# Five of eight loads moved from Sync's DMA queue to GpSimd's software queue in a 3-D average pooling kernel

## Chip, cores and metric

One NeuronCore of a Trainium2 chip. The metric is the device time of one execution in microseconds (us). Times are medians of several runs in the fast state, with a granted clock of 1.0, apart from x8_late_store, a single run whose state is unknown.

## The reference

```python
def setup_inputs():
    batch, channels, d, h, w = (8, 32, 32, 32, 32)
    kernel_size = 2
    return {'x': np.random.randn(batch, channels, d, h, w).astype(np.float32), 'kernel_size': kernel_size}

# cut here: reference() loops over i, j, k; in short:
# result[:, :, i, j, k] = mean of the 2 x 2 x 2 window of x at (2i, 2j, 2k)
```

The input is 256 rows (batch x channels) of 128 KiB, 33.55 MB; the output is an eighth of that, 4.19 MB.

## The kernel before

Each group of 128 rows fills the 128 partitions. A load brings 16, 32 or 48 KiB of every row into a slot of one ring buffer; the vector engine (DVE) then adds along d, along w and along h. Slots are reused, so some loads must wait until DVE has finished with the slot. DVE reports its progress by a count: one for each tile's first addition, one for its second and one for the read at its end, so three a tile.

```python
    plan = [                 # (row group, first KiB, KiB, slot in the ring)
        (0, 0, 32, 0),
        (0, 32, 48, 32),
        (0, 80, 48, 80),
        (1, 0, 32, 128),
        (1, 32, 32, 0),
        (1, 64, 32, 32),
        (1, 96, 16, 64),
        (1, 112, 16, 80),
    ]
    # ... pool_unit: three DVE operations and one read of an accumulator
    for t, k0, kb, r0 in plan:
        unit = ring[:, r0 * KF:(r0 + kb) * KF]
        nc.sync.dma_start(out=unit, in_=xv[t * P:(t + 1) * P, k0 * KF:(k0 + kb) * KF])
        pool_unit(unit, t, k0, kb)

    for t, k0, kb in [(0, 0, 16), (1, 0, 12), (1, 12, 4)]:
        nc.sync.dma_start(out=ov[...], in_=obuf[t][...])
```

After the program is built, it is edited: the first store is held back until one DVE count before the second store's (17 instead of what its data needs), and the first load is moved ahead of the opening barrier.

```python
    need, = [w for w in second.sync_info.on_wait if w.ant_name.startswith("DVE")]
    # ... in the first store's waits:
            w = copy.replace(w, wait_value=need.wait_value - 1)
```

## Time and profile before

| | before |
|---|---|
| time, median | 91.19 us (91.16 to 91.21, 3 runs) |
| span of the profile | 88.0 us |
| DVE busy | 63.2 us |
| DMA queue, share of 16 engines | 99.1% |
| last load landed / last store landed | 80.1 / 89.9 us |

"Landed" is the last of the 16 semaphore counts that the DMA engines post for a transfer. The span ends with the last instruction, before the last store has landed. In the windows view used below, a row gives a stretch of time and its length, DVE's busy time and instructions, GpSimd's (POOL), the granted clock, the mean busy share of the 16 DMA engines, and GB/s. (A packet is counted in the stretch where it starts, so a share can pass 1.) Here is its tail before:

```profile
69.60:73.40 3.80, 3.03 (x1) 0.00 (x0) 1.00 1.03 440
73.40:78.00 4.60, 4.53 (x3) 0.00 (x0) 1.00 1.00 427
78.00:80.00 2.00, 2.00 (x3) 0.00 (x0) 1.00 0.98 418
80.00:85.00 5.00, 4.90 (x6) 0.00 (x0) 1.00 1.01 431
```

The reader should see the second-last column: the engines never rest, through the last loads and over the change to stores near 80.

### The profile page before, as it was taken

To read this page: it belongs to the slowest core of one execution; us is meant where nothing else is said; L and a number is where in the kernel's file an instruction comes from. 1 tells how busy PE (TensorE), PEld (TensorE's weight loads), DVE (VectorE), ACT (ScalarE), POOL (GpSimd) and SP (SyncE) were. 2 spreads that over 40 slices of the span, in tenths; PEclk is the share of its full clock that TensorE was granted. 3 is DMA by queue.
4 is the path that set the end of the run, shared out by engine and by line. 5 is a ranking of instruction groups with operands and counts; after the bars stand their busy time and mean duration, and the time that the engine had idled before them with its cause. 6 is when DMAs were issued, how large, how long until landed. Compare 5 with 4: busy or idle time off the path is not lost.

```text
span 88.0 us, 78 instructions
## 1 busy us (share of the span) xinstructions
DVE 63.2 (72%) x32; POOL 0.2 (0%) x4
## 2 busy tenths in 40 slices
DVE  0000049991008999942999999999999299999994
POOL 0000000000000000000000000000000000000000
DMA  8979999888998889986999988999989999999999
GB/s 238 462 328 402 477 402 670 358 358 358 536 536 358 358 358 603 469 358 298 417 477 477 477 358 358 477 477 477 402 358 432 417 417 462 402 447 440 410 434 400
DMA packets 1440, 37.26 MB, mean 424 GB/s; under 512 B 152, under 2 KB 152, under 8 KB 160
## 3 DMA queue, kind: packets, MB, share of 16 engines
q1 hardware_dynamic: 1440, 37.26, 99.1%
HBM read 33.55 MB, written 4.19 MB: 429 GB/s over the span
## 4 chain that ended last, share of the span: by engine, by line
DMA 66%; DVE 32%; issue 0%; DVEq 0%
DMA ring<-in_x_dram 66%; DVE ring L60 18%; DVE ring L65 9%; DVE obuf L68 5%; DVE dummy L68 0%; DVEq L91 0%
## 5 line engine op out<-in xcount | busy, mean ns | idle before, releaser
L60 DVE TENSOR_TENSOR ring<-ring 128x4096 f32<-128x4096 f32 (+2 forms) x8 | 35.4, 4422 | 23.0 <-DMA ring<-in_x_dram 23.0
L65 DVE TENSOR_TENSOR ring<-ring 128x2048 f32<-128x2048 f32 (+2 forms) x8 | 18.3, 2292 | 0.3
L68 DVE CUSTOM_DVE_ANT_1 obuf<-ring 128x1024 f32<-128x1024 f32 (+2 forms) x8 | 9.8, 1225 | 0.3
L68 DVE DVE_READ_ACCUMULATOR2_ANT dummy<- 128x1 f32 x8 | 0.7, 82 | 0.0
L183 POOL MEMSET const-bfloat16-1.0<- 128x1 bf16 x1 | 0.1, 103 | 0.0
L183 POOL MEMSET const-uint8-127<- 128x1 uint8 x1 | 0.1, 102 | 0.0
L183 POOL MEMSET const-float32-0.0<- 128x1 f32 x1 | 0.1, 100 | 0.2 <-issue 0.2
L183 POOL MEMSET const-float32-1.0<- 128x1 f32 x1 | 0.1, 99 | 0.0
## 6 DMA issues: line engine op xcount, KB each, us to landing
ring<-in_x_dram SPq DMA_DIRECT2D x4, 4096.0 KB, 36.2
ring<-in_x_dram SPq DMA_DIRECT2D x2, 6144.0 KB, 32.9
ring<-in_x_dram SPq DMA_DIRECT2D x2, 2048.0 KB, 32.7
out_dram<-obuf SPq DMA_DIRECT2D x1, 2048.0 KB, 7.9
out_dram<-obuf SPq DMA_DIRECT2D x1, 1536.0 KB, 10.2
out_dram<-obuf SPq DMA_DIRECT2D x1, 512.0 KB, 3.1
```

What stands on the lines that cost most here:

```text
L60: first = nc.vector.tensor_add(out=b.rearrange("p (o e) -> p o e", o=od), in0=a[:, :, 0], in1=a[:, :, 1])
L65: nc.vector.tensor_add(out=c, in0=bv[:, :, 0], in1=bv[:, :, 1])
L68: nc.vector.tensor_tensor_reduce(out=obuf[t][:, o0:o0 + od * 256].rearrange("p (j k) -> p j k", k=16), in0=cv[:, :, 0], in1=cv[:, :, 1], s ...
L183: nc = _bacc.Bacc("TRN2", target_bir_lowering=False, num_devices=1)
```

## The change

Its intent, as I read it, is to give each of the five middle loads one large packet per DMA engine instead of eight. I call the first load of SP (the Sync engine) H0 (32 KiB a row), GpSimd's five S0 to S4 (48, 48, 32, 32, 32 KiB), and SP's last two H1 and H2 (16 KiB each).

```diff
     plan = [
-        (0, 0, 32, 0),
-        (0, 32, 48, 32),
-        (0, 80, 48, 80),
-        ...
+        (0, 32, 48, 32, False),      # S0, now first on DVE
+        (0, 0, 32, 0, True),         # H0, still issued first
+        (0, 80, 48, 80, False),      # S1
+        (1, 0, 32, 128, False),      # S2
+        (1, 32, 32, 0, False),       # S3, in H0's slot
+        (1, 64, 32, 32, False),      # S4, in S0's slot
+        (1, 96, 16, 64, True),       # H1
+        (1, 112, 16, 80, True),      # H2
     ]
...
+        if hw:
+            nc.sync.dma_start(out=unit, in_=src)
+        else:
+            nc.gpsimd.dma_start(out=unit, in_=src, single_packet=True)
...
+    n, load = loads[1]               # H1
+            w = copy.replace(w, wait_value=14)   # its wait for DVE, raised to count 14
```

So three things change at once: the queue, DVE's order of the first two tiles, and a raised wait of H1.

More of the change, by code (lines that the diff above doesn't have):

```diff
@@ L44, in pool_rows @@
     plan = [
-        (0, 0, 32, 0),
-        (0, 32, 48, 32),
-        (0, 80, 48, 80),
-        (1, 0, 32, 128),
-        (1, 32, 32, 0),
-        (1, 64, 32, 32),
-        (1, 96, 16, 64),
-        (1, 112, 16, 80),
+        (0, 32, 48, 32, False),
[6 more added lines that the diff above has]
+        (1, 112, 16, 80, True),
     ]
@@ L72, in pool_unit @@
         )
-    for t, k0, kb, r0 in plan:
+    for t, k0, kb, r0, hw in plan:
         unit = ring[:, r0 * KF:(r0 + kb) * KF]
-        nc.sync.dma_start(out=unit, in_=xv[t * P:(t + 1) * P, k0 * KF:(k0 + kb) * KF])
+        src = xv[t * P:(t + 1) * P, k0 * KF:(k0 + kb) * KF]
+        if hw:
+            nc.sync.dma_start(out=unit, in_=src)
+        else:
+            nc.gpsimd.dma_start(out=unit, in_=src, single_packet=True)
         pool_unit(unit, t, k0, kb)
@@ L93 @@
     program = blocks[tc.starting_block_idx].instructions
+    loads = [
+        (n, i) for n, i in enumerate(program)
+        if isinstance(i, mybir.InstDMACopy) and "in_" in i.ins[0].memref
+        and i.engine == nc.sync.engine]
+    assert len(loads) == 3
+    n, load = loads[1]
+    waits = []
+    for w in load.sync_info.on_wait:
+        if w.ant_name.startswith("DVE"):
+            assert w.wait_value < 14
+            w = copy.replace(w, wait_value=14)
+        waits.append(w)
+    program[n] = copy.replace(load, sync_info=mybir.SyncInfo(
+        on_wait=waits, on_update=load.sync_info.on_update))
     stores = [
@@ L113 @@
     opening = blocks[0].instructions
-    load = next(i for i in program if isinstance(i, mybir.InstDMACopy))
+    load = next(
+        i for i in program if isinstance(i, mybir.InstDMACopy) and i.engine == nc.sync.engine)
     assert load.engine == nc.sync.engine
```

## The prediction

> **What bounds the kernel now.** I read the page first (busy share of the vector engine DVE, and the share of the 16 DMA engines), then the timeline (when each tile's first addition could start, which is when its load had landed), then the chain that ended last. The page:
>
> ```profile
> DVE 63.2 (72%) x32; POOL 0.2 (0%) x4
> ...
> q1 hardware_dynamic: 1440, 37.26, 99.1%
> HBM read 33.55 MB, written 4.19 MB: 429 GB/s over the span
> ```
>
> One queue keeps all 16 DMA engines busy for 99.1% of the 88.0 us span; DVE needs 63.2 us. So DMA is the bound. The reader should see in the third column of the queue line that no idle is left to remove: only bytes, packet overhead or the ends of the run can give time back.
>
> The timeline shows the landings, as the ends of DVE's idle times:
>
> ```profile
> 12.14 4.42 DVE L60 TENSOR_TENSOR ring<-ring 128x4096 f32<-128x4096 f32 x1 [12.14 <-DMA ring<-in_x_dram]
> ...
> 26.65 6.56 DVE L60 TENSOR_TENSOR ring<-ring 128x6144 f32<-128x6144 f32 x1 [6.49 <-DMA ring<-in_x_dram]
> ...
> 41.21 6.56 DVE L60 TENSOR_TENSOR ring<-ring 128x6144 f32<-128x6144 f32 x1 [2.81 <-DMA ring<-in_x_dram]
> ...
> 70.37 4.42 DVE L60 TENSOR_TENSOR ring<-ring 128x4096 f32<-128x4096 f32 x1 [1.54 <-DMA ring<-in_x_dram]
> ```
>
> From 12.14 to 26.65 one load of 128 x 48 KiB (6.29 MB) lands: 434 GB/s. From 41.21 to 70.37 three loads of 128 x 32 KiB (12.58 MB) land in 29.16 us: 432 GB/s. The stream has no holes. The chain that ended last has this tail:
>
> ```profile
> 38.43 31.91 DMA ring<-in_x_dram
> 70.35 0.02 issue
> 70.37 4.43 DVE ring L60
> ...
> 82.58 2.22 DVE ring L60
> 84.80 0.02 issue
> 84.83 1.24 DVE ring L65
> 86.06 0.02 issue
> 86.08 0.69 DVE obuf L68
> ```
>
> After the sixth load lands at 70.35, DVE works without a break to 86.78 on three tiles. The last store (0.5 MB, issued at 86.8, 3.1 us to landing) ends at 89.9; the median time, 91.19, is 1.3 later. Meanwhile DMA is full too (the trace's semaphore landings: last load 80.1, stores 85.0, 88.7, 89.9), so the DVE tail and the byte stream end nearly together.
>
> **What the Trainium skill says.** (1) "DMA: Bandwidth & Descriptors", section "Issuing engines are not separate DMA queues": DMAs from Sync and GpSimd run on the same 16 engines and interleave, so a second queue adds no bandwidth. The trace agrees in so far as one queue already fills 99.1%. (2) Same page, "Queues, rings and completion order": each engine round-robins between the rows with work, a whole packet at a time. The trace before has one queue, so nothing shows it; this decides the rivals below. (3) Same page, "Why small descriptors are slow (HBM only)": a fixed overhead of some 3 cycles per packet. The trace agrees in kind: its packets of 16,384, 32,768 and 49,152 bytes take 611, 1213 and 1815 ns (medians). The slope, (1815-611)/32768, is 27.2 GB/s; what is left over is about 9 ns a packet. (4) "SBUF — State Buffer", "Who interferes with whom": GpSimd's descriptor writing is locked out by DVE's two-port modes, and the page infers that a tensor_tensor doesn't lock it out, because that takes only the shared read side. No GpSimd DMA has run yet, so no run shows it.
>
> **The change part by part.** Bytes, tiles and DVE instructions are the same: the instruction order shows 33 working DVE rows in another order (the 48-KiB tile first, the 32-KiB tile second), five loads moved from SP to GpSimd.
>
> Removed: packet boundaries. A load has 128 rows, 8 per engine, so 8 packets an engine become 1. Five loads x 7 packets x 9 ns = 0.3 us per engine. That is all that the byte stream can gain.
>
> Removed and added issue time: five issues of 0.33 to 0.52 us on SP become GpSimd's. Each lies under a 10 to 14 us transfer, so 0.
>
> Moved: SP's first load (call it H0) still starts before the barrier at 0.00, first packet at 1.02. GpSimd's first load (S0, 48 KiB rows) can be issued after the barrier, about 0.8 (SP's second load was at 0.80 before). I allow 2 to 3 us for software descriptors, my estimate. By 4.0 H0 has done about two of its eight rows (the first took 1.7 to 2.2 us in the trace, later ones 1.22). Then S0's single packet holds each engine for 8 x 1.806 = 14.45 us.
>
> My main line supposes that H0 then gets its six rows before S1, as the changed DVE order implies. Landing is 0.4 us after the last byte, as before. Tile times from the timeline: 48 KiB 11.7 us (26.65 to 38.40), 32 KiB 7.9 (52.88 to 60.81), 16 KiB 4.2 (78.30 to 82.50).
>
> - S0 lands 18.9, H0 26.2, S1 40.6, S2 50.3.
> - DVE: S0 18.9 to 30.6, H0 30.6 to 38.5, S1 40.6 to 52.3, S2 52.3 to 60.2.
> - S3 reuses H0's slot: issued at 38.5, well before S2 has left the engines (49.9), lands 60.0. S4 reuses S0's slot and lands 69.6.
> - DVE: S3 60.2 to 68.1, S4 69.6 to 77.5.
> - The penultimate SP load now waits for the 14th DVE count. Three counts per tile (the first store before waited for count 17 and started at 77.15, as the sixth tile's second addition ended), so 14 is S3's second addition, about 66.9. That is 2.4 us before S4 leaves the engines at 69.3: just in time. The last two loads land about 74.6 and 79.5, DVE ends 85.9.
> - Stores: 2, 1.5 and 0.5 MB behind the loads, last landing about 89.5, against 89.9.
>
> Sum: 91.19 minus 0.3 for packets, perhaps 0.1 more or less at the start: 90.8. The DVE tail gets about 0.9 us of air (85.9 against 86.8), but the byte stream then sets the end, so that air isn't gained.
>
> **The rivals.**
>
> A. Strict alternation of one packet per queue. H0's rows are packets of 32 KiB, S0 to S2 packets of 384, 384 and 256 KiB an engine. H0 then gets one row after S0, one after S1, and the rest after S2: it lands near 50. DVE, in program order, idles from 30.6 to 50; S3 is issued only at 58. DVE from 50 on has 7.9 + 11.7 + 7.9 x 3 + 4.2 x 2 = 51.7 us: ends near 102, last store 3.1 later, plus 1.3: about 106. For it: the skill's words on round robin. Against it: the changed wait at count 14 would then fall near 84, with DMA idle since about 70; nobody who saw that trace would set it there, while in my main line it fits to 2 us. That is an argument from the design, not a measurement.
>
> B. The queues share by bytes, or H0 goes first entirely. S0 lands at 25 (equal shares: 604 KiB left of both at 27.2 GB/s from 3 us) or 26.6 (H0 first). DVE starts there and has 63.4 us: ends 88.5 to 90.0, plus 3.1 plus 1.3: 93 to 94.4, slower by 2 to 3.5%. DVE becomes the bound. For it: DVE's start moves from 12.1 to 18.9 at best, so only about 4 us of DVE slack is left (23.0 us of idle before, of which 18.9 is now spent before the first addition). Against it: the reordering would make no sense.
>
> C. Software descriptors are slower: a gap of a microsecond between two GpSimd packets, or a descriptor write held up by DVE. Five gaps of 1 us add up to 5 us at most; but other queued work can fill part. I think 0 to 2 us.
>
> D. Faster by more than 2%: needs under 89.4. At the pure slope of 27.2 GB/s an engine (435 GB/s) 37.75 MB take 86.8 us; with 1.0 to the first packet, 0.4 to land and 1.3 after, that is 89.5 with every packet overhead gone. So practically excluded.
>
> **Range and chances.** Main line 90.8 (about 70%, with C's small gaps up to 92), B about 10%, A about 12%, C large about 8%. I put the prediction at 91.0 and the range at 90.4 to 93.5; A lies outside. Faster by over 2%: 0.02; within 2% (89.4 to 93.0): 0.74; slower: 0.24.
>
> **What would show it.** Right: two DMA queues with about 25 MB on the software one and a joint share near 99%; DVE's first addition near 19, second tile without a long wait (landing by 27 to 31); single software packets of about 14.4 us; the last two loads issued near 67; DVE ending near 86. Wrong by A: DVE idle some 20 us before the second tile, DMA share falling between 50 and 60. Wrong by B: first addition at 25 or later and an unbroken DVE after it. Wrong by C: the DMA share a few per cent lower in the middle slices, with idle DVE before the third and later tiles. The prediction is wrong altogether if engines deliver more than 27.2 GB/s in single packets, for which the trace shows no sign.

## The result

| | before | after |
|---|---|---|
| time, median | 91.20 us (91.16 to 91.26, 4 runs) | 97.06 us (96.94 to 97.09, 4 runs) |
| DVE busy | 63.2 us | 63.1 us |
| DVE starts its first addition | 12.14 us | 26.44 us |
| S4 landed (sixth load before) | 70.35 us | 70.07 us |
| last load landed | 80.1 us | 85.9 us |
| last store landed | 89.9 us | 95.7 us |

The ratio is 1.064, 95% interval 1.0621 to 1.0658. Ratios here are the mean time of one kernel's fast runs over that of the other's of the same rounds, so not quite the ratio of the medians quoted. Executions over 1.5% slower than the fastest of the same kernel are left out of the means.

The page after:

```profile
DVE 63.1 (69%) x32; POOL 3.0 (3%) x9
...
q0 software_dynamic: 720, 25.17, 63.8%
q1 hardware_dynamic: 635, 11.21, 31.1%
HBM read 33.55 MB, written 4.19 MB: 413 GB/s over the span
```

The two queues together keep the engines busy for 94.9% of the span instead of 99.1%. The software queue carried exactly its 25.17 MB, in 720 packets: 5 loads x 128 rows is 640 data packets, plus 80 semaphore writes. In spite of the one-packet flag, the records show every row by itself. (A row is one partition's piece of a load, 8 of them per engine; it is not the queue row of the skill's page.)

Where does DVE start? The timeline after:

```profile
26.44 6.56 DVE L60 TENSOR_TENSOR ring<-ring 128x6144 f32<-128x6144 f32 x1 [26.44 <-DMA ring<-in_x_dram]
...
38.11 4.42 DVE L60 TENSOR_TENSOR ring<-ring 128x4096 f32<-128x4096 f32 x1
```

Only the first addition has a bracket: DVE waits for 26.44 us, and from then on data are there, apart from 0.14 us before H2's tile near 85.9. In the trace's landings H0 was complete at 22.8, before S0 at 26.4, but DVE takes S0 first. How the queues shared is in the DMA view after, for the stretch from 7 to 20 us (packets, MB, share):

```profile
q0 software_dynamic: 64, 3.15, 55.9%
q1 hardware_dynamic: 66, 2.16, 38.5%
```

In that stretch 64 rows of S0 and 66 of H0 began: one row for one row. The bytes differ only because S0's rows are 48 KiB and H0's 32.

And the end of the chain that ended last, after (start, us, what):

```profile
70.10 2.30 DVE ring L65
72.40 0.02 issue
72.42 0.33 SPq L78
...
72.87 13.04 DMA ring<-in_x_dram
85.90 0.02 issue
85.93 2.30 DVE ring L60
```

Count 14 comes at 72.4 with the end of the fifth tile's second addition (L65). Only then SP issues H1 and H2, and H2 takes 13.0 us to land. The windows after show what that does to DMA:

```profile
69.60:73.40 3.80, 3.73 (x3) 0.00 (x0) 1.00 0.07 17
73.40:81.00 7.60, 7.53 (x5) 0.00 (x0) 1.00 1.00 405
81.00:85.00 4.00, 3.97 (x4) 0.00 (x0) 1.00 0.97 287
```

Two losses stand here, to be held against the same stretch of the kernel before. From 69.6 to 73.4 DMA runs dry (17 GB/s): S4's last row ends at 69.63 and H1's first begins at 73.38. And from 81 to 85 the engines are "busy" but move only 287 GB/s: rows of 16 KiB, every one of which took 0.611 us in the kernel before, take up to 1.32. A busy share near 1 is thus not a full rate. DVE is hardly held up by this: it ends at 90.2, and the last store is issued at 90.24. But the stores stand behind the late loads, so this store takes 5.4 us to land instead of 3.1.

### The profile page after: what moved, and what is told of

Its sections match the earlier page's. It is cut to its first block, busy times and chain, and to the rows that moved or that the text cites. A ratio compares the mean times of both kernels' runs of the same rounds, so it can differ in the third digit from the quotient of the medians.

```text
span 91.3 us, 78 instructions
## 1 busy us (share of the span) xinstructions
DVE 63.1 (69%) x32; POOL 3.0 (3%) x9
## 3 DMA queue, kind: packets, MB, share of 16 engines
q0 software_dynamic: 720, 25.17, 63.8%
## 4 chain that ended last, share of the span: by engine, by line
DVE 55%; DMA 42%; issue 1%; SPq 0%; PEldq 0%; DVEq 0%
DMA ring<-in_x_dram 42%; DVE ring L60 31%; DVE ring L65 16%; DVE obuf L68 7%; SPq L78 0%; DVE dummy L68 0%; PEldq L95 0%; DVEq L95 0%
## 5 line engine op out<-in xcount | busy, mean ns | idle before, releaser
L60 DVE TENSOR_TENSOR ring<-ring 128x4096 f32<-128x4096 f32 (+2 forms) x8 | 35.4, 4423 | 26.6 <-DMA ring<-in_x_dram 26.4
L65 DVE TENSOR_TENSOR ring<-ring 128x2048 f32<-128x2048 f32 (+2 forms) x8 | 18.3, 2293 | 0.3
L80 POOL DMA_DIRECT2D ring<-in_x_dram x5 | 2.7, 554 | 44.3 <-DVE dummy L68 43.4
## 6 DMA issues: line engine op xcount, KB each, us to landing
ring<-in_x_dram SPq DMA_DIRECT2D x1, 4096.0 KB, 22.8
```

Of the source, the lines that this page charges most:

```text
L60: first = nc.vector.tensor_add(out=b.rearrange("p (o e) -> p o e", o=od), in0=a[:, :, 0], in1=a[:, :, 1])
L65: nc.vector.tensor_add(out=c, in0=bv[:, :, 0], in1=bv[:, :, 1])
L80: nc.gpsimd.dma_start(out=unit, in_=src, single_packet=True)
```

## The experiments

My theory after the result (Theory 1): rows of the two queues alternate, so S0 lands at 26.4; DVE starts there because its order puts S0 first; the late DVE makes the count-14 wait late, and DMA runs dry. Rivals: the software queue is slow by itself (Theory 2), or the one-packet flag sets how the queues share (Theory 3). The first eight runs below were made on one chip and the last two on another, each beside runs of the kernel before on the same chip.

### x1_tile_order: DVE takes H0 first

```diff
     plan = [
-        (0, 32, 48, 32, False),
         (0, 0, 32, 0, True),
+        (0, 32, 48, 32, False),
```

> The changed kernel with one thing undone: DVE takes the 32-KiB tile (SP's first load) first and the 48-KiB tile (GpSimd's first load) second; all loads, queues and the count-14 wait stay. Theory 1 (the loss is the DVE order: GpSimd's rows alternate with SP's, so the tile that DVE waits for lands at 26.4 instead of 18.9): DVE starts near 22.8, fourteenth count near 68.7, so no hole before the last two loads, end near 91.0. Theory 2 (the software queue itself is slow): little gained, 95 or more.

Measured: 93.74 us (93.4 to 93.85, 5 fast runs; a sixth, 95.04, counts as slow), ratio to before 1.0271 (1.0254 to 1.0289). DVE starts at 22.88 and count 14 comes at 68.86, both as expected. So the hole all but closes, and 3.3 us come back. But the expected 91.0 was missed by 2.7. The windows of this run say where:

```profile
69.60:73.40 3.80, 3.66 (x3) 0.00 (x0) 1.00 0.97 349
73.40:78.00 4.60, 4.53 (x3) 0.00 (x0) 1.00 0.99 424
78.00:82.00 4.00, 3.93 (x5) 0.00 (x0) 1.00 1.02 328
```

DMA restarts at 69.84 after a pause of 0.1 us or more on each engine, and its first rows cost 0.56 us more than usual per engine (349 GB/s). Then from 78 to 82 there are slow rows again (1.0 us per engine in the packet records). H2 lands at 82.7 instead of 80.1.

### x2_gate12: H1 waits for count 12 instead of 14

```diff
-            w = copy.replace(w, wait_value=14)
+            w = copy.replace(w, wait_value=12)
```

> The changed kernel with the wait of SP's second load lowered from DVE count 14 to 12. Theory 1: DVE still starts at 26.4 and works without a break, the two loads are issued at 65.7 instead of 72.4, the hole of 3.8 us in the DMA stream goes, DVE ends near 89.8 and the last store ends the run 3.1 later: 94.2. That splits the loss of 5.9 into some 3 for the start and some 3 for the wait. Theory 2 (software queue): about 97 still.

Measured: 94.14 us (94.1 to 94.34, 4 runs), ratio 1.0326 (1.0307 to 1.0345). It came out as Theory 1 said, to 0.1 us. H1 is issued at 65.9, the loads end by 80.0 without slow rows, and DVE, which started at 26.57, sets the end. The stretch that ran dry in the changed kernel (0.07, 17 GB/s) is full here:

```profile
69.60:73.40 3.80, 3.73 (x3) 0.00 (x0) 1.00 1.06 453
```

The last store is issued at 90.14, only 0.1 us earlier than in the changed kernel, but lands 2.7 us later and not 5.4: what the late wait costs is paid in the queue of stores, not in DVE's time. Theory 2 in its simple form (about 97 still) falls.

### x4_many_packets: without the one-packet flag

```diff
-            nc.gpsimd.dma_start(out=unit, in_=src, single_packet=True)
+            nc.gpsimd.dma_start(out=unit, in_=src)
```

> The changed kernel without the one-packet flag on the five GpSimd loads. Theory 1 (the flag doesn't make a packet hold an engine; rows of the two queues alternate either way): first tile lands at 26 again, time 97.1 plus at most 0.3, rows of 49,152 bytes at 1.815 us again. Theory 3 (the flag sets how the queues share): another landing order or time, by 1 us or more.

Measured: 96.90 us (96.82 to 97.01, 4 runs), ratio 1.0625 (1.0609 to 1.0641). Its DMA view from 7 to 20 us:

```profile
q0 software_dynamic: 64, 3.15, 55.8%
q1 hardware_dynamic: 65, 2.13, 37.9%
```

Row for row again, 64 to 65. Median rows took 1.815 us (48 KiB) and 1.213 us (32 KiB) with the flag and without it. So the flag neither holds an engine nor saves the time between rows here, and Theory 3 falls. Whether the flag took effect in the descriptors at all, the records do not show: they have 720 packets on this queue either way. S2 to S4 landed 9.71 us apart with the flag and 9.73 without.

### x5_before_48_first: the tile order alone, on SP's queue

```diff
-    for t, k0, kb, r0 in plan:
-        ... load and pool each tile in turn
+    first, second = load(0), load(1)
+    pool_unit(*second)
+    pool_unit(*first)
+    for n in range(2, len(plan)):
+        pool_unit(*load(n))
```

> The kernel before, all eight loads on SP's queue in the old order, but DVE takes the second load's 48-KiB tile first. No software queue in it. Theory 1: DVE starts at 26.65 and then has 63.3 us without a break, ends at 90.0, plus 3.1 for the last store and 1.3: 94.4, with the DMA stream unbroken to the last load at 80.1. Theory 2 (queue, not order): about 91.2 to 92.

Measured: 94.21 us (94.15 to 94.31, 4 runs), ratio 1.033 (1.0314 to 1.0345). Without any GpSimd DMA, starting DVE with the second load costs 3.0 us, the same as in x2_gate12 (3.0). The reason for that part is DVE's start, not the queue.

### x7_order_gate13: both undone, software queue kept

The tile order of x1_tile_order, and H1's wait at count 13.

```diff
-            w = copy.replace(w, wait_value=14)
+            w = copy.replace(w, wait_value=13)
```

> The tile-order kernel (DVE takes SP's first tile first) with the wait of SP's second load lowered from count 14 to 13, so that it is issued near 66.5, while GpSimd's last load still runs. The tile-order run missed its 91.0 by 2.7 us: its trace has three 16-KiB rows per engine at 0.9 to 1.25 us instead of 0.61, shortly after the first store was issued, and a slow first row after 69.6. Theory R (both come from letting the DMA engines run dry and restarting them together): gone here, time 90.8 to 91.0. Theory S (the first store's arrival, at 77, disturbs load rows queued ahead of it): here the last load is nearly done by 77, so also nearly gone: 91.0 to 91.5. Theory 2 (the software queue costs something by itself): 92 or more.

Measured: 91.39 us (91.26 to 91.55, 6 runs), ratio 1.0018 (1.0003 to 1.0033). No restart and no slow rows:

```profile
60.00:69.60 9.60, 9.50 (x6) 0.00 (x0) 1.00 1.00 430
69.60:73.40 3.80, 2.65 (x3) 0.00 (x0) 1.00 1.00 427
73.40:78.00 4.60, 4.53 (x3) 0.00 (x0) 1.00 1.04 445
78.00:82.00 4.00, 3.97 (x4) 0.00 (x0) 1.00 0.98 418
```

All five loads still run on GpSimd's queue with the flag, and the time is 0.2% above that of before. It lies in the range of Theory S, not in Theory R's. The four kernels make a table of two by two:

| | H1 at count 14 | H1 at count 12 or 13 |
|---|---|---|
| DVE takes S0 first | 97.06 | 94.14 |
| DVE takes H0 first | 93.74 | 91.39 |

With the early count, the tile order is worth 2.75 us; with S0 first, the count is worth 2.9. They add up to nearly all of the 5.9, and what remains for the software queue is 0.2. The two are not independent: taken in the other order they are worth 2.35 (the count, with H0 first) and 3.3 (the order, at count 14), because a later DVE also makes the count later.

### x3_no_gate: H1's added wait removed

```diff
-            w = copy.replace(w, wait_value=14)
```

> The changed kernel without the added wait at count 14: SP's last two loads are issued as soon as their slots are free, near 38 and 58, and share the engines row by row with GpSimd's loads. Theory 1 (rows alternate): GpSimd's fifth load lands near 79 to 80 instead of 70.1, DVE, which takes it sixth, idles some 5 to 6 us from 73.6, and ends near 95.6: about 100. If one GpSimd load held an engine as one packet, the SP rows would come between the loads only: its fifth load would land near 73, and the time be about 94.

Measured: 100.55 us (100.52 to 100.6, 4 runs), ratio 1.1024 (1.1009 to 1.104). DVE waits for S3 and for S4 (landed 80.1):

```profile
68.57 4.42 DVE L60 TENSOR_TENSOR ring<-ring 128x4096 f32<-128x4096 f32 x1 [2.64 <-DMA ring<-in_x_dram]
80.11 4.42 DVE L60 TENSOR_TENSOR ring<-ring 128x4096 f32<-128x4096 f32 x1 [3.52 <-DMA ring<-in_x_dram]
```

The expectation had all of the idle time ahead of S4; it was split between two tiles, with a sum of 6.2 us, near the expected 5 to 6. The DMA view of this run from 58 to 70 us, while H2 and GpSimd's loads overlap:

```profile
q0 software_dynamic: 112, 3.15, 60.8%
q1 hardware_dynamic: 112, 1.84, 35.7%
```

Again 112 to 112. This shows that rows alternate here too, and what the raised wait spares: without it SP's loads take engine time from GpSimd's, and the time is 3.5 us longer than with it.

### The slow rows: x6, x8, x9, x10

Two questions were left: what the restart costs, and what makes load rows slow near the end.

**x6_before_hole** is the kernel before, SP alone, with an added wait of the seventh load for count 16, so that DMA runs dry near 70.

```diff
+    n, late = loads[6]
+    program[n] = copy.replace(late, sync_info=mybir.SyncInfo(
+        on_wait=list(late.sync_info.on_wait) + [copy.replace(dve, wait_value=16)],
+        on_update=late.sync_info.on_update))
```

> The kernel before, SP's queue alone, with an added wait: the seventh load is issued only at DVE count 16 (near 74.8), so that DMA runs dry from 70 to about 75.8. It tells what a hole costs without any software queue. Loads would land near 86.6, the stores' bytes follow until 96.4, time 97.7 without slow rows. Theory S: slow rows come 1.4 us after the first store's issue at 77.15, so from 78.5 on, in the middle of the two loads, and the time is about 99. Theory R (a set time after the restart, 8.4 us as in the changed kernel): slow rows from 84.2 on. If no slow rows: they belong to the software queue.

Measured: 99.34 us (99.19 to 100.03, 4 runs), ratio 1.0917 (1.0885 to 1.0949).

```profile
70.00:75.60 5.60, 5.34 (x2) 0.00 (x0) 1.00 0.00 0
75.60:84.00 8.40, 4.74 (x4) 0.00 (x0) 1.00 1.01 406
84.00:87.00 3.00, 2.08 (x4) 0.00 (x0) 1.00 1.01 262
```

The slow rows come at 84 to 87, without a software queue. So they don't belong to it. That moment fits Theory R, which had them from 84.2 on. They did not come at 78.5, soon after the first store's issue at 77.0, as Theory S had it.

**x8_late_store** is the changed kernel with its first store held until count 21.

```diff
-            w = copy.replace(w, wait_value=need.wait_value - 1)
+            w = copy.replace(w, wait_value=need.wait_value + 3)
```

> The changed kernel with the first store held back from DVE count 17 to 21 (from 80.35 to about 85.7), so that no store is issued while the last two loads run. Theory S: no slow rows, the last load lands at 84.0 on all engines (85.0 to 85.9 in the changed kernel). Theory R: slow rows again from 81.9 on, landing up to 85.9. The time itself gets worse either way, about 98, as DMA then waits for the stores.

Measured: 98.68 us in a single run (state unknown). The packet records have the slow first rows (0.46 us per engine) but none later; H2 lands at 84.2 to 84.5 instead of 85.0 to 85.9.

```profile
73.40:81.00 7.60, 7.53 (x5) 0.00 (x0) 1.00 0.99 397
81.00:84.00 3.00, 2.96 (x4) 0.00 (x0) 1.00 0.92 393
84.00:86.80 2.80, 2.77 (x4) 0.00 (x0) 1.00 0.00 0
```

So Theory R (a fixed time after the restart) does not hold in this profile, and it points to a store queued behind the loads as a condition of the slow rows. It is one run, so this is weaker than the rest. In each run so far that had slow rows, there had also been a restart. The next run separates the two.

**x9_before_early_store** is the kernel before without its own delay of the first store.

```diff
-            w = copy.replace(w, wait_value=need.wait_value - 1)
```

> The kernel before without its own delay of the first store: it is issued as soon as its tile half is done, near 53, and then stands queued behind the last loads, on SP's queue alone, with no hole and no restart. So far slow rows came at the end of the last load where DMA had restarted AND a store had been queued 3 us or more before the loads ended; the two always went together. Theory P (a store queued early is enough): three slow rows near 78 to 80, the last load lands near 81.3 instead of 80.1, time 92.2 to 92.8. Theory R2 (the restart is needed): no slow rows, 91.2.

Measured: 92.18 us (92.09 to 92.24, 4 runs), ratio 1.0113 (1.0096 to 1.013). The store is issued at 52.9. There is no restart, and yet from 77 to 82, where the kernel before had an even rate, this run has:

```profile
77.00:82.00 5.00, 4.93 (x5) 0.00 (x0) 1.00 0.95 370
```

Against it the kernel before:

```profile
77.00:82.00 5.00, 4.90 (x6) 0.00 (x0) 1.00 1.02 436
```

In this run sixteen rows of 16 KiB are slowed by 0.39 us on average, and the last load lands at 80.6 to 81.0 instead of 79.7 to 80.1. Theory P holds in kind: no restart is needed, and the early store costs 1.0 us of time. Its size is not explained: three slow rows per engine were expected, the records show 0.4 us per engine in all, and 0.3 us was already lost when the sixth load landed (70.64 against 70.35), in part through rows that were slow before the store was issued.

**x10_order_store18** is x1_tile_order with the first store at count 18.

```diff
-            w = copy.replace(w, wait_value=need.wait_value - 1)
+            w = copy.replace(w, wait_value=need.wait_value)
```

> The tile-order kernel (93.74) with the first store one DVE count later, 18 instead of 17, so issued at 78.3 instead of 77.0, some 1.7 us before the last load would end at 80.0; the restart near 69.7 stays. Theory P: fewer or no slow rows, last load at 80.5 to 81.5 instead of 82.7, time 92.0 to 93.0. Theory R2: slow rows as before, 93.7.

Measured: 92.13 us, but spread from 91.34 to 92.64 over 4 runs; ratio 1.01 (1.0043 to 1.0156). The median is in Theory P's range. The profile is of the fastest run, though, and in it S0's first row began only at 6.4 (5.3 in x1_tile_order), H0 landed at 21.3 (22.9), H1 was issued at 67.7, and DMA never ran dry. So this profile can't tell P from R2, and the run only agrees with P.

Not settled: why queued stores slow the load rows ahead of them, and whether a restart makes it worse (0.8 to 1.2 us per engine in the packet records with a restart and an early store, in the changed kernel, x1_tile_order, x4_many_packets and x6_before_hole; 0.4 in x9_before_early_store).

## Why the prediction was wrong

1. **The bound** was read rightly: DMA full for the whole span, DVE with little air. DVE's tile times held (11.7, 7.9 and 4.2 us).
2. **The step that failed** is "Then S0's single packet holds each engine for 8 x 1.806 = 14.45 us", with what followed: H0's rest before S1, S0 at 18.9. The runs showed row-by-row alternation instead (64 to 66 rows with the flag, 64 to 65 without), S0 at 26.4 and H0 at 22.8. S0's start was mis-sized as well: I had it on the engines by 4.0, and its first rows began at 5.3 to 6.7. DVE therefore started 7.5 us later than predicted. I had allowed about 4 us of air for it, so DVE became the bound: that is worth 2.75 to 3.0 us (x7_order_gate13 against x2_gate12; x5_before_48_first).
3. **Rival B had the landing right** (S0 at 25 to 26.6) but not the time, and the landing by luck: the queues shared by rows, not by bytes (3.15 MB to 2.16 from 7 to 20 us), and H0 did not go first entirely. Its sum was off too: 604 KiB at 27.2 GB/s from 3 us on end at 25.7, not 25. It put 93 to 94.4, which is what x2_gate12 measured (94.14), not what the change gave. What it left out is that count 14 moves with DVE: from 66.9 to 72.4, after S4's last row at 69.63. Hole, slow restart and slow rows cost the other 2.9 us. A wait on another engine's progress has to be re-timed in every rival, not only in the main line.
4. **The weight of B was wrong because of an argument from design**: "the reordering would make no sense", "nobody who saw that trace would set it there". The order and the count fitted my main line to 2 us, and I took that as evidence for how the engines share.
5. **The gain of 0.3 us** from removed packet boundaries did not come: rows took 1.815 and 1.213 us with the flag and without, and the records show 640 row packets. S4 landed 0.3 us earlier than the sixth load before, but 0.2 of that was there at the second load already (26.42 against 26.63).
6. **Rivals A and C**: A's strict alternation is what ran, with rows of both queues as its packets; its H0 near 50 needed S0's single packets and fell with them. C fell to 0.2 us, in x7_order_gate13. D stayed excluded. (The 33 working DVE rows in the prediction are 32 in both pages.)

The sum for the last store's landing, 95.66 against 89.88: S4's last row ends 0.37 us earlier (69.63 against 69.995), the hole takes 3.75, the first rows after it about 0.5, the slow rows about 1.2. The 0.7 that remains of the 5.78 lies in the rest of the tail; part of it is that the engines no longer end together (H2's 16 landings spread over 0.9 us instead of 0.4). It was not tested by itself.

## What to carry to other kernels

A second DMA queue doesn't come behind or ahead of the first: what it had ready took turns with it row by row in these runs (64 rows to 66), so decide in which order tiles will be complete before fixing the order of the engine that consumes them. A transfer gated on an engine's progress is only as well placed as that engine's start; when the start moves, look at the DMA share just before the gated transfer. Where loads end and stores begin, try the time of the first store's issue: issuing it early cost 1.0 us in x9_before_early_store, while issuing it so late that DMA had to wait for it gave 98.68 us against 97.06 in the single run of x8_late_store.

## What the Trainium skill lacked or had wrong

- "DMA: Bandwidth & Descriptors", "Queues, rings and completion order", says that engines take turns between queues a packet at a time. The runs agree if each row is a packet (64 to 66, 112 to 112 rows), but the page does not tell that asking for one packet per load leaves rows alternating: 97.06 us with the flag, 96.90 without.
- The same page, "Latency and other measured facts", gives a first byte after about 1 us for software queues and 0.6 us for hardware ones. Here S0's issue began at 1.30 and its first row at 5.34, 4.0 us later, of which at most 1.2 can be waiting for one of H0's rows; SP's first rows began 1.0 us after their issue (0.00 to 1.01, and 72.42 to 73.38).
- No page that I found has that load rows get slow when a store is queued behind them: 1.0 us of time in x9_before_early_store (92.18 against 91.15), and in the changed kernel, where a restart came before, 16-KiB rows at up to 1.32 us instead of 0.611.
- No page that I found gives the cost of letting the engines run dry beyond the gap itself: about 0.5 to 0.7 us per engine in the first rows (after, x1_tile_order, x4_many_packets, x6_before_hole, x8_late_store).
- "SBUF — State Buffer", "Who interferes with whom", only infers that a tensor_tensor leaves descriptor writing alone. The trace agrees as far as the issue goes: GpSimd's issues took 0.53 us both with DVE idle (at 1.96) and beside its addition (at 46.42).
